# One block of a feed-forward product, instead of two, goes pair by pair: a transformer step on one core

## The chip, the core and the metric

The kernel runs on one core of one Trainium2 chip, in one launch. The metric is device time in microseconds (us). Three runs of the kernel before gave a median of 1669.56 us (1669.26 to 1672.01). Engines are named as in the profile: PE multiplies matrices, ACT and DVE are the scalar and the vector engine, POOL is GpSimd, and SP's queue issues most of the transfers (ACT issues some).

## What is computed

The reference is one layer of a diffusion backbone on 1152 tokens (1024 latent, 128 context) of width 1024, all in float32. Cut to what matters here:

```python
mix = (sigmoid(ga) * attn + sigmoid(gc) * conv) @ w_o           # 1024 x 1024
x = LN(ALPHA * x + g1 * mix)                                      # first norm
h = x * (1 + sc2) + sh2                                           # modulation
f = square(relu(h @ w1 + b1)) @ w2 + b2                           # 1024 -> 4096 -> 1024
x = LN(ALPHA * x + g2 * f)                                        # second norm
```

The change sits between `@ w_o` and the beginning of `h @ w1`; attention, convolution and the second product are not touched.

## The kernel before

**Float32 by parts.** PE multiplies a rounded format. Each float32 operand is cut into a high part (a copy on ACT) and a low part (a subtraction on DVE, source minus high part), and each product is three matmuls: high by high, high by low, low by high. So whatever PE reads has first been through one ACT and one DVE instruction.

**The wo passes.** The output projection goes over nine tiles of 128 tokens in three passes: half 0 of the columns for tiles 0 to 5, half 1 for tiles 0 to 8, half 0 for tiles 6 to 8 (`PASSES`). A tile is 8 x 3 matmuls of 512 columns. The weights of a pass are four entries of 512 KB, which come through a ring with two raw buffers and three buffers of parts (a fourth pair, `wo_last`, is given in for the last entry). `ring.load_to` loads an entry as soon as a raw buffer is free, which is when its last split (the DVE subtraction at line 122) has run. So of a pass's four entries two can be loaded ahead, and the other two only once the first two have been split; the splits of a new pass run beside the last tile of the pass before, as each entry's old parts come free.

**Work beside the passes.** `todo` is a list of closures with costs, written by hand; `spend(0.69)` after every third matmul runs as many as fit. They are: `ln1_sum` (lines 1046, 1047 and 1050 on DVE: gate, residual, statistics of half a tile), `ln1_apply` (norm of a tile: DVE and ACT by turns, two passes of ACT at line 1058), `turn` (four 128x128 transposes on PE at line 1112 into one bank, taken out with modulation by ACT at line 1122), and `combine` (the operands of the next stage: ACT's high parts at line 1130, DVE's low parts at line 1140 and sums at line 1144).

**The first feed-forward product** is done by a Strassen-Winograd scheme: both operands are quartered, and seven products (A11 B11, S1 T1, S2 T2, A12 B21, S3 T3, S4 B22, A22 T4, with S and T sums of quarters of the weights and of the tokens) take the place of eight. The hidden width is cut into 16 blocks j; the tokens into two pairs of quarter tiles of 288 columns. A product of one block with one pair is 12 matmuls. Products accumulate in four accumulators X, V, Z, W: in the order of `PARTS`, X, V, X, Z, X, V, W. After a product its accumulator is copied out (`keep`, ACT, line 1364) or added to a kept copy (`plus`, DVE, line 1367), and X and V go on accumulating afterwards, so the next product into X waits for the copy.

**The first blocks.** The operands of the second pair need tiles 4 to 8, so they come late. `AHEAD = 2` blocks are therefore done first with pair 0 alone and then with pair 1 alone: blocks 0 and 1 on pair 0, blocks 0 and 1 on pair 1, and blocks 2 to 15 with both pairs. Their weights' parts (14 products, hi and lo, 256 KB each) are cut long before, during the convolution stage, and kept in DRAM (`w1d`); each is loaded twice, once for each pair (line 1188). From block 2 on, `w1_load` (line 1173) loads the raw weights of a block, 1 MB, and sums and parts are made four products ahead (`w1_prep`, lines 824, 1195, 1196).

**Beside the four half blocks** run the rest of `todo`: the last norms, the turns of tiles 4 to 8 for pair 1 through two banks, and `combine(1)`, which is taken up product by product: `while pairs[-1] == 1 and made <= k`. Hidden results are squared (lines 1320, 1321), summed (line 1324) and spilled to DRAM by transfers that ACT issues.

Of the kernel before, what the change touches and what calls it, by code (L numbers as in the profile page):

```python
# [144 lines left out]
def emit(nc, tc, ctx, aps, outs):  # L145
# [654 lines left out]
    HALVES = (slice(0, 512), slice(512, 1024))  # L800
    WPARTS = ("A11", "S1", "S2", "A12", "S3", "S4", "A22")
# [8 lines left out]
    def w1_sum(u, pool):  # L810
# [9 lines left out]
        t = w1sum[j, 2] if name == "S4" else tmp(pool, [P, 512], "S1" if name == "S3" else name, 1)  # L820
# [6 lines left out]
    AHEAD = 2  # L827
    w1d = [dram.tile([P, 2, 512], F32, name=f"w1d{u}") for u in range(7 * AHEAD)]

    def w1_ahead():  # L830
# [9 lines left out]
        def high(u):  # L840
            if st:
                keep(u - 1)
# [8 lines left out]
        def keep(u):  # L851
            for i, x in enumerate(st.pop(u)):
                dma(w1d[u][:, i], f32(x))

        for j in range(AHEAD):
            bg.append(lambda j=j: load(j))
            for u in range(7 * j, 7 * j + 7):
                bg.extend([lambda u=u: high(u), lambda u=u: low(u)])
            bg.append(lambda: keep(max(st)))
# [229 lines left out]
    def place(pair, store):  # L1089
        for name in PARTS:  # L1090
            own = {"T4": "q00", "T3": "q10", "B22": "q01"}.get(name) if pair else None
            hx[pair][name] = (next(store), own or next(store))
# [11 lines left out]
    def turn(t, pair, half):  # L1104

        def go():
# [12 lines left out]
            for i in range(4):  # L1119
                kb = 4 * half + i  # L1120
                for x, y, n in pieces:
                    act(raw[pair][half][x // PT][:, i, x % PT:x % PT + n], b[:, i * P + y:i * P + y + n], AF.Identity,
                        scale=m2col[:, cond, 1, kb:kb + 1], bias=m2col[:, cond, 0, kb:kb + 1])
        return go

    def combine(pair):

        def high(name, src):
            for h_, k0, n in hx[pair][name][0]:
                nc.scalar.copy(h_, src[:, k0:k0 + n])  # L1130

        def low(name, src):
            hi, lo = hx[pair][name]
            if isinstance(lo, str):
                lo = [(tmp(rawp, [P, 4, PT], lo, 1, F32R), 0, 4)]
                hx[pair][name] = hi, lo
# [17 lines left out]
        if pair == 0:  # L1154
            first, second, third = cuts("B11", b11), cuts("B21", b21), cuts("B22", b22)
            t1, t3, t2, t4 = cuts("T1", b11), cuts("T3", b12), cuts("T2", b11), cuts("T4", b21)
            return ([first[0], second[0], first[1]] + sums(b11, b12, b11) + [t1[0], second[1], third[0], t1[1]]
                    + sums(b11, b22, b11) + [t2[0]] + sums(b21, b21, b11) + [t4[0], t2[1], third[1], t4[1]]
                    + sums(b12, b22, b12) + t3)
# [6 lines left out]
    BLOCKS = [(j, (p,)) for p in range(2) for j in range(AHEAD)] + [(j, (0, 1)) for j in range(AHEAD, NJ)]  # L1166
# [9 lines left out]
    def w1_prep(s_):  # L1176

        if s_ >= 7 * len(BLOCKS) or s_ in w1part:
            return
        j, k = BLOCKS[s_ // 7][0], s_ % 7  # L1180
        u = 7 * j + k
        if s_ // 2 not in wtile:
            wtile[s_ // 2] = [ringp.tile([P, 1024], F32R, tag=t, name=f"w1{t}{s_}", bufs=3) for t in ("whi", "wlo")]
        hi, lo = (t[:, HALVES[s_ % 2]] for t in wtile[s_ // 2])
        w1part[s_] = hi, lo
        if j < AHEAD:
            for i, x in enumerate((hi, lo)):
                dma(f32(x), w1d[u][:, i])
        else:
            w1_load(j)  # L1190
            w1_sum(u, wsp)
            if k < 6:
                w1_sum(u + 1, wsp)
            src = w1sum[j, k]
            nc.scalar.copy(hi, src)
            vec.tensor_tensor(out=lo, in0=src, in1=f32(hi), op=ALU.subtract)
        if k == 6 and s_ // 7 + 1 >= 2 * AHEAD:
            w1_load(j + 1 if j >= AHEAD else AHEAD)
# [5 lines left out]


# [25 lines left out]
    def put_turn(t, pair):  # L1231
        todo.extend((0.4, turn(t, pair, half)) for half in range(2))

    for ps, (half, ts_) in enumerate(PASSES):
        if ps == 0:
            ring.given[ring.nuse + 3] = wo_last(f"o{ps}")
        w = [ring.take(ahead=0) for _ in range(4)]
        for t in ts_:
# [7 lines left out]
            for kb in range(KB):  # L1246
# [4 lines left out]
                if t == ts_[-1] and kb % 2:  # L1251
                    if ps == 2:
                        if kb < 7:
                            w1_prep(kb - 1)
                            w1_prep(kb)
                    else:
                        if kb == 7:
                            ring.given[ring.nuse + 3] = wo_last(f"o{ps + 1}")
                        ring.split_to(ring.nuse + kb // 2 + 1)
                        ring.load_to(len(seq))  # L1260
                        room[0] -= 1.2
                spend(0.69)
# [4 lines left out]
            if ps == 1 and 1 <= t < 6:  # L1267
                put_turn(t - 1, 0)
            if ps == 1 and t == 5:
                store = segments(act_tiles(0) + act_tiles(1), 0)  # L1270
                store = list(store) + [single(hx0, n) for n in range(4)]
                place(0, iter(store))
                todo.append((0.0, lambda: todo.extendleft(reversed(combine(0)))))
# [4 lines left out]
    for _ in range(2):  # L1278
        todo.popleft()[1]()
    put_turn(7, 1)  # L1280
    put_turn(8, 1)
# [5 lines left out]
    turn_banks.extend(lambda i=i: bank(i) for i in (6, 7))  # L1287
# [9 lines left out]
    def dbank(tag, j, pairs):  # L1297

        if len(pairs) == 1:
            return bank("XVZW".index(tag)).rearrange("p (a b) -> p a b", a=1)  # L1300
        return ps1.tile([P, 2, 512], F32, tag=tag, name=f"d{tag}{j}", bufs=1)

    def w1_mm(b, s_, name, first, pairs):

        hi, lo = w1part[s_]
# [29 lines left out]
    def second_pair():  # L1335

        nonlocal made
# [3 lines left out]
        place(1, iter(store + [single(hx1, 4 + n) for n in range(6)]))  # L1341

        def count():
            nonlocal made
            made += 1

        for closures in combine(1):
            todo.extend(closures + [(0.0, count)])

    store = list(segments(act_tiles(2), 0))  # L1350
    todo.append((0.0, second_pair))
    B = {}
    for n, (j, pairs) in enumerate(BLOCKS):
        sl = slice(pairs[0], pairs[-1] + 1)
        bias = [b1c[:, j + i * NJ:j + i * NJ + 1] for i in range(2)]
        c1, c5, c2, c3 = (ht(t, n)[:, sl] for t in ("c1", "c5", "c2", "c3"))
        h = {m: ht("h" + m, n)[:, sl] for m in ("11", "22", "12", "21", "T2", "T3", "T4")}
# [11 lines left out]
        def spill(name, t, j=j, sl=sl):  # L1369
            nc.scalar.dma_start(hd[name, j][:, sl], t)  # L1370

        def finish(h=h, j=j, sl=sl, spill=spill):
# [5 lines left out]
            def parts(name, t):  # L1378
                hi = tmp(t1p, [P, 2, PT], "hi" + name, 1, F32R)[:, sl]
                nc.scalar.copy(hi, t)  # L1380
                vec.tensor_tensor(out=t.bitcast(F32R), in0=t, in1=f32(hi), op=ALU.subtract)
                late.append(lambda: (nc.scalar.dma_start(hd[name, j][:, sl, 0], f32(hi)),
                                     nc.scalar.dma_start(hd[name, j][:, sl, 1], t)))
# [10 lines left out]
        for k in range(7):  # L1394
            s_ = 7 * n + k
# [4 lines left out]
            while pairs[-1] == 1 and made <= k and todo:  # L1400
                todo.popleft()[1]()
# [8 lines left out]
            elif k == 3:  # L1410
                plus(h["11"], b, c1)
            elif k == 4:
                keep(c3, b, 1)
                plus(h["22"], b, c5)
            elif k == 5:
                plus(h["12"], b, c2)
            elif not last:
                plus(h["21"], b, c3)
            if last and k == 6:
                break  # L1420
            if todo:
                spend(1.3)
# [3 lines left out]
            elif k == 4:  # L1426
                after(lambda h=h, spill=spill: (square(h["22"]), spill("B11", h["11"])))
# [434 lines left out]
```

## Time and profile before

| | us |
|---|---|
| median of three runs | 1669.56 |
| the profiled execution | 1671.68 |
| its span | 1669.9 |
| PE busy | 1599.8 |
| DVE busy | 1026.0 |
| ACT busy | 734.8 |
| POOL busy | 201.4 |

The span counts from the first to the last instruction of the profiled execution; the run's own time lies 1.8 us above it. PE's matmuls overlap, so its busy share is no measure of its speed: the spacing of starts is. A wait names what ended it. In the views a line number is that of the kernel before.

### The profile page before, as it was taken

The numbers are of one execution on the slowest core, as the hardware profiler recorded it, in microseconds if no ns is written. First come the engines' busy times: TensorE is split into PE (matmuls) and PEld (weight loads), VectorE is DVE, ScalarE is ACT, GpSimd is POOL, SyncE is SP. The second block draws the span as 40 slices with busy tenths as digits, with TensorE's granted clock in tenths as the row PEclk, the third lists the DMA queues.
The fourth block names the chain that finished last, engine by engine and source line by source line (L and its number), as shares of the span: only waits on it lengthen the run. The fifth ranks groups of instructions, "written<-read, shape, count | busy, mean of one in ns | idle before, by whom it ended". The sixth has DMA issues, their size and how long they took to land.

```text
span 1669.9 us, 27468 instructions
## 1 busy us (share of the span) xinstructions
PE 1599.8 (96%) x10432; PEld 1539.7 (92%) x10432; DVE 1026.0 (61%) x1793; ACT 734.8 (44%) x1408; POOL 201.4 (12%) x214
## 2 busy tenths in 40 slices
PE   7999999999999999999987799999999999999995
PEld 5799999999999999997767799999999999999995
DVE  6568888665565554345464555666666457865666
ACT  5367777511112122232557555655565335453030
POOL 2145556100000002210000000000000121000002
PEclk9999999999999999999998999999999999999998
DMA  8432222133332223533326845444557898777792
GB/s 313 143 90 73 57 62 54 57 114 108 108 95 80 79 76 91 175 102 120 132 89 222 293 143 171 153 168 160 171 174 273 292 327 277 228 258 237 230 328 88
DMA packets 157419, 267.63 MB, mean 160 GB/s; under 512 B 41392, under 2 KB 62000, under 8 KB 157288
## 3 DMA queue, kind: packets, MB, share of 16 engines
q1 hardware_dynamic: 125352, 218.68, 40.9%
q10 hardware_dynamic: 31936, 47.21, 7.9%
q8 instruction: 82, 1.34, 0.3%
q14 instruction: 49, 0.40, 0.1%
HBM read 198.94 MB, written 66.88 MB: 159 GB/s over the span
## 4 chain that ended last, share of the span: by engine, by line
PE 77%; DVE 8%; DMA 5%; ACT 5%; issue 3%; SPq 1%; POOL 0%; ACTq 0%; POOLq 0%; DVEq 0%
PE ps L363 8%; PE ps L365 8%; PE ps L361 7%; PE pq L1552 6%; PE pq L1553 6%; PE pq L1554 6%; PE dX L1312 3%; PE dX L1314 3%; PE dX L1313 3%; PE dV L1312 2%; PE dV L1314 2%; PE dV L1313 2%; PE ps L880 2%; PE ps L881 2%; PE ps L882 2%
## 5 line engine op out<-in xcount | busy, mean ns | idle before, releaser
L365 PE MATMUL ps<-ahi,wl 128*128 128x384 f32 x864 | 292.7, 339 | 0.9 <-DVE wl L122 0.9
L363 PE MATMUL ps<-alo,wh 128*128 128x384 f32 x864 | 292.5, 339 | 0.0
L361 PE MATMUL ps<-ahi,wh 128*128 128x384 f32 x864 | 292.5, 339 | 0.0
L1552 PE MATMUL pq<-xh,vh 128*128 128x288 f32 x640 | 190.3, 297 | 3.2 <-ACT accc L1647 2.6
L1553 PE MATMUL pq<-xl,vh 128*128 128x288 f32 x640 | 189.5, 296 | 0.0
L1554 PE MATMUL pq<-xh,vl 128*128 128x288 f32 x640 | 188.9, 295 | 0.0
L365 PEld LDWEIGHTS ps<-ahi,wl 128*128 128x128 f32 x864 | 162.5, 188 | 1.7 <-DVE wl L122 1.5
L361 PEld LDWEIGHTS ps<-ahi,wh 128*128 128x128 f32 x864 | 162.4, 188 | 1.4 <-issue 0.2
L363 PEld LDWEIGHTS ps<-alo,wh 128*128 128x128 f32 x864 | 162.5, 188 | 0.8
L1552 PEld LDWEIGHTS pq<-xh,vh 128*128 128x128 f32 x640 | 120.6, 188 | 3.7 <-ACT accc L1647 2.8
L1554 PEld LDWEIGHTS pq<-xh,vl 128*128 128x128 f32 x640 | 121.2, 189 | 0.0
L1553 PEld LDWEIGHTS pq<-xl,vh 128*128 128x128 f32 x640 | 120.7, 189 | 0.0
L1519 DVE TENSOR_TENSOR xl<-hraw,xh 128x576 fp32r<-128x576 f32 x80 | 60.4, 755 | 77.4 <-ACT xh L1515 77.2
L122 DVE TENSOR_TENSOR wl<-wr,wh 128x1024 fp32r<-128x1024 f32 (+1 forms) x54 | 60.9, 1130 | 70.2 <-ACT wh L109 69.9
L1515 ACT CAST xh<-hraw 128x576 fp32r<-128x576 f32 x80 | 53.8, 673 | 96.7 <-issue 39.1
L1699 POOL TENSOR_TENSOR xm<-xm,ag 128x1024 f32<-128x1024 f32 x9 | 22.5, 2497 | 607.6 <-DMA w2r<-w 545.0
L743 DVE SCALAR_TENSOR_TENSOR acc<-wmb,sil,acc 128x512 f32<-128x512 f32 x112 | 78.2, 748 | 12.3 <-DMA wmb<-wmb 12.2
L109 ACT CAST wh<-wr 128x1024 fp32r<-128x1024 f32 (+1 forms) x62 | 58.2, 950 | 46.9 <-PE ps L1250 28.7
L1312 PE MATMUL dX<-hxahi,w1whi 128*128 128x288 f32 x224 | 67.5, 301 | 5.5 <-DVE h L1367 5.5
L563 ACT ACTIVATE s<-s,st 128x512 f32<-128x512 f32 (+1 forms) x72 | 49.6, 689 | 51.7 <-DVE st L561 51.1
L1314 PE MATMUL dX<-hxahi,w1wlo 128*128 128x288 f32 x224 | 67.0, 299 | 0.0
L881 PE MATMUL ps<-acl,wh 128*128 128x384 f32 x192 | 64.2, 334 | 0.0
(351 smaller groups left out, 4355.2 us busy)
## 6 DMA issues: line engine op xcount, KB each, us to landing
w2r<-w SPq DMA_DIRECT2D x144, 256.0 KB
hraw<-hdT SPq DMA_DIRECT2D x60, 288.0 KB
wmb<-wmb SPq DMA_DIRECT2D x64, 256.0 KB
w1r<-w SPq DMA_DIRECT2D x28, 512.0 KB
hraw<-hdB SPq DMA_DIRECT2D x44, 288.0 KB
hdB<-h ACTq DMA_DIRECT2D x42, 288.0 KB
hdT<-hT ACTq DMA_DIRECT2D x42, 288.0 KB
mr<-wma SPq DMA_DIRECT2D x16, 512.0 KB
```

What stands on the lines that cost most here:

```text
L122: engine.tensor_tensor(out=lo[:, :w], in0=self.raw.pop(i)[:, :w], in1=hi.bitcast(F32)[:, :w], op=ALU.subtract)
L361: mm(b[:, :CH], lhsT=hi[:, ws], rhs=a[0][:, kb, :], start=first and kb == 0, stop=False)
L363: mm(b[:, :CH], lhsT=hi[:, ws], rhs=a[1][:, kb, :], start=False, stop=False)
L365: mm(b[:, :CH], lhsT=lo[:, ws], rhs=a[0][:, kb, :], start=False, stop=last and kb == n - 1)
L743: vec.scalar_tensor_tensor(out=a, in0=t, scalar=sil[:, k, cond:cond + 1], in1=a, op0=ALU.mult, op1=ALU.add)
L881: mm(b[:, :CH], lhsT=hi[:, ws], rhs=parts[kb][1][:, cs_], start=False, stop=False)
L1312: mm(o, lhsT=hi[:, ws], rhs=xh, start=first and kb == 0, stop=False, **kw)
L1313: mm(o, lhsT=hi[:, ws], rhs=xl, start=False, stop=False, **kw)
L1314: mm(o, lhsT=lo[:, ws], rhs=xh, start=False, stop=kb == 3, **kw)
L1552: mm(o, lhsT=hi[:, ws], rhs=xh[:, i], start=j == 0, stop=False)
L1553: mm(o, lhsT=hi[:, ws], rhs=xl[:, i], start=False, stop=False)
L1554: mm(o, lhsT=lo[:, ws], rhs=xh[:, i], start=False, stop=j == NJ - 1)
```

## The change

Only block 0 goes pair by pair: block 0 on pair 0, block 0 on pair 1, then blocks 1 to 15 with both pairs. Its seven products' weight parts are cut early and kept in DRAM as before, but loaded once: six products fill the ring's three buffers, the seventh lies in two tiles that the hidden results use later. The products of every block come in a new order (`ORDER`: A11 B11, A12 B21, S1 T1, S2 T2, S4 B22, S3 T3, A22 T4), hence the accumulators in the order X, Z, V, X, V, X, W. Raw weights of wo's third and fourth entry are loaded into tiles of the hidden results (`wo_more`), which are free until then. Half, or a quarter, of the evictions of each turn move from ACT to DVE (`n_vec`), the turns of the first feed-forward stage use four banks instead of two, the cuts of pair 0's B11 and B21 begin after tile 3 instead of tile 5, no work is handed out during the last tile of the first two passes, and what goes beside each product of block 0 on pair 0 is written out (`beside`). Squares, sums and spills of block 0 are done once for both pairs.

```diff
+    ORDER = (0, 3, 1, 2, 5, 4, 6)
...
-        t = w1sum[j, 2] if name == "S4" else tmp(pool, [P, 512], "S1" if name == "S3" else name, 1)
+        t = tmp(pool, [P, 512], {"S4": "S1", "S3": "S2"}.get(name, name), 1)
...
-    AHEAD = 2
-    w1d = [dram.tile([P, 2, 512], F32, name=f"w1d{u}") for u in range(7 * AHEAD)]
+    w1d = [dram.tile([P, 2, 512], F32, name=f"w1d{u}") for u in range(7)]
...
-    def turn(t, pair, half):
+    def turn(t, pair, half, n_vec=0):
...
+                    if i < 4 - n_vec:
+                        act(to_, from_, AF.Identity, scale=sc, bias=sh)
+                    else:
+                        vec.tensor_scalar(out=to_, in0=from_, scalar1=sc, scalar2=sh, op0=ALU.mult, op1=ALU.add)
...
-        return [cuts("B11", b11), sums(b11, b12, b11) + cuts("T1", b11), sums(b11, b22, b11) + cuts("T2", b11),
-                cuts("B21", b21) + sums(b21, b21, b11), sums(b12, b22, b12) + cuts("T4", b21) + cuts("T3", b12),
-                cuts("B22", b22), []]
+        t1, t2, t3, t4, b = cuts("T1", b11), cuts("T2", b11), cuts("T3", b12), cuts("T4", b21), cuts("B22", b22)
+        return [cuts("B11", b11), cuts("B21", b21),
+                sums(b11, b12, b11) + [t1[0], b[0]] + sums(b12, b22, b12) + [t1[1]],
+                sums(b11, b22, b11) + [t2[0], b[1], t2[1]] + sums(b21, b21, b11) + [t4[0]], [], [t4[1]] + t3, []]
-    BLOCKS = [(j, (p,)) for p in range(2) for j in range(AHEAD)] + [(j, (0, 1)) for j in range(AHEAD, NJ)]
+    BLOCKS = [(0, (0,)), (0, (1,))] + [(j, (0, 1)) for j in range(1, NJ)]
...
+        if s_ < 7 or 14 <= s_ < 7 * len(BLOCKS):
...
+            if j == 0:
+                for x, t in enumerate((hi, lo)):
+                    dma(f32(t), w1d[k][:, x])
+                return
...
+    def wo_more(set_):
+        for e in (2, 3):
+            n = base + 4 * set_ + e
+            k, half = 2 * e, (0, 1, 0)[set_]
+            ts_ = [tmp(t1p, [P, 2, PT], "h" + ("11", "22", "12", "21")[2 * (e - 2) + x], 1)
+                   .rearrange("p a b -> p (a b)")[:, :512] for x in range(2)]
+            for x, t in enumerate(ts_):
+                dma(t, aps["wo"][k + x][:, HALVES[half]])
+            wo_raw[n] = ts_
...
+        for x, y in zip(src, HALVES):
+            nc.scalar.copy(hi[:, y], x)
+            vec.tensor_tensor(out=lo[:, y], in0=x, in1=f32(hi)[:, y], op=ALU.subtract)
...
-        w = [ring.take(ahead=0) for _ in range(4)]
+        w = [wo_take() for _ in range(4)]
+        if ps < 2:
+            wo_more(ps + 1)
+        else:
+            w1_load(1)
...
-                spend(0.69)
+                if ps == 2 or t < ts_[-1]:
+                    spend(0.69)
+                elif kb == 0:
+                    todo.popleft()[1]()
+                    room[0] = -1.0
...
-    turn_banks.extend(lambda i=i: bank(i) for i in (6, 7))
+    turn_banks.extend(lambda i=i: bank(i) for i in (0, 1, 6, 7))
...
+    beside = {0: [fn for _, fn in todo], 1: [last_norm, turn(7, 1, 0, 2), turn(7, 1, 1, 2), lambda: pair_parts(0)],
+              2: [lambda: pair_parts(1)],
+              3: [turn(8, 1, 0, 2), turn(8, 1, 1, 2), second_pair], 4: [lambda: pair_parts(2)],
+              5: [lambda: pair_parts(3)]}
...
-            while pairs[-1] == 1 and made <= k and todo:
-                todo.popleft()[1]()
+            while n == 1 and made <= min(i + 1, 6):
+                pair_parts(made)
...
+            if n == 0:
+                for fn in beside.get(i, ()):
+                    fn()
+                continue
```

More of the change, by code (lines that the diff above doesn't have):

```diff
@@ L849, in low, with keep_all @@
             vec.tensor_tensor(out=lo, in0=w1sum[u // 7, u % 7], in1=f32(hi), op=ALU.subtract)
[L851 to L859, printed above, removed]
+        def keep_all():
+            while st:
+                u, parts = st.popitem()
+                for i, x in enumerate(parts):
+                    dma(w1d[u][:, i], f32(x))
+        bg.append(lambda: load(0))
+        for u in ORDER:
+            bg.extend([lambda u=u: high(u), lambda u=u: low(u)])
+        bg.append(keep_all)
     gemv_rest()
@@ L1087, in act_tiles, with place @@
         return [actp.tile([P, KB * CH], F32R, tag=tag, name=f"hx{tag}{n}", bufs=NCH) for tag in ("ahi", "alo")]
[L1089 to L1092, printed above, removed]
+    def place(pair, store, names=PARTS):
+        for name in names:
+            own = ({"T4": (None, "q00"), "T3": ("q10", "q11")} if pair else {}).get(name, (None, None))
+            hx[pair][name] = tuple(x or next(store) for x in own)
     def single(pool, n):
@@ L1231, in put_turn @@
     def put_turn(t, pair):
-        todo.extend((0.4, turn(t, pair, half)) for half in range(2))
+        n_vec = 2 if not pair or t > 5 else 1
+        todo.extend((0.4 * n_vec, turn(t, pair, half, n_vec)) for half in range(2))
     for ps, (half, ts_) in enumerate(PASSES):
@@ L1268, in emit @@
                 put_turn(t - 1, 0)
+            if ps == 1 and t == 3:
+                store = list(segments(act_tiles(0), 0))
+                place(0, iter(store), ("B11", "B21"))
+                todo.append((0.0, lambda: todo.extendleft(reversed(combine(0)[0]))))
             if ps == 1 and t == 5:
[L1270 to L1273, printed above, removed]
+                store = store[4:] + list(segments(act_tiles(1), 0)) + [single(hx0, n) for n in range(4)]
+                place(0, iter(store), [x for x in PARTS if x not in ("B11", "B21")])
+                todo.append((0.0, lambda: todo.extendleft(reversed(combine(0)[1]))))
                 put_turn(4, 1)
@@ L1277, in emit @@
                 put_turn(6, 1)
-    for _ in range(2):
-        todo.popleft()[1]()
-    put_turn(7, 1)
-    put_turn(8, 1)
+    todo.popleft()[1]()
+    last_norm = todo.popleft()[1]
     sln.close()
@@ L1335, in second_pair @@
     def second_pair():
-        nonlocal made
         spill_x()
@@ L1378, in parts @@
             def parts(name, t):
[L1379 removed]
+                hi = tmp(t1p, [P, 2, PT], "hi" + name, 1, F32R)
                 nc.scalar.copy(hi, t)
                 vec.tensor_tensor(out=t.bitcast(F32R), in0=t, in1=f32(hi), op=ALU.subtract)
[L1382 to L1383 removed]
+                late.append(lambda: (nc.scalar.dma_start(hd[name, j][:, :, 0], f32(hi)),
+                                     nc.scalar.dma_start(hd[name, j][:, :, 1], t)))
             parts("B21", h["21"])
@@ L1392, in sums @@
             diff(h["T2"], h["22"], h["12"])
-        for k in range(7):
-            s_ = 7 * n + k
+        for i, k in enumerate(ORDER):
+            s_ = 7 * n + i
             new = {0: "X", 1: "V", 3: "Z", 6: "W"}.get(k)
```

140 lines of the change are left out of this document (88 added, 52 removed).

## The prediction

> **What bounds the kernel now.** I began with the page: who is busy, and at what clock.
>
> ```profile
> span 1669.9 us, 27468 instructions
> PE 1599.8 (96%) x10432; PEld 1539.7 (92%) x10432; DVE 1026.0 (61%) x1793; ACT 734.8 (44%) x1408; POOL 201.4 (12%) x214
> PEclk9999999999999999999998999999999999999998
> ```
>
> PE is the bound, and the number of its matmuls doesn't change. The change can therefore only give back time in which PE stood or ran at a lower clock. The next view is busy time by stretch: the three wo passes, the four half blocks (cut in two), the beginning of block 2, and blocks 2 to 15. The columns are PE, weight loads, DVE, ACT, POOL, the granted clock, the DMA share and GB/s.
>
> ```profile
> 762.90:801.00 38.10, 35.01 (x145) 27.99 (x145) 20.24 (x28) 5.13 (x6) 1.52 (x2) 0.96 0.35 118
> 801.00:857.70 56.70, 55.17 (x258) 44.43 (x256) 28.92 (x49) 34.27 (x74) 0.00 (x0) 1.00 0.40 138
> 857.70:880.80 23.10, 18.78 (x72) 13.96 (x72) 17.62 (x25) 8.03 (x10) 0.00 (x0) 0.93 0.35 106
> 880.80:920.00 39.20, 30.15 (x175) 28.18 (x173) 16.80 (x26) 31.18 (x76) 0.00 (x0) 0.83 0.63 216
> 920.00:958.40 38.40, 28.66 (x206) 27.33 (x204) 20.11 (x35) 18.51 (x39) 0.00 (x0) 0.99 0.90 306
> 958.40:964.20 5.80, 5.75 (x24) 5.75 (x25) 5.08 (x10) 2.84 (x6) 0.00 (x0) 0.51 0.39 122
> 964.20:1264.00 299.80, 299.80 (x2253) 299.80 (x2253) 184.17 (x277) 175.35 (x282) 0.00 (x0) 1.00 0.47 161
> ```
>
> From 964 on PE never stands; all that the change can save lies between 763 and 964. To see how much, I need PE's undisturbed pace. These are rows of the timeline (two successive tiles of a wo pass, then the first matmul of two blocks that lie 12 apart) and, third, one turn pair from the chain of waits.
>
> ```profile
> 779.30 0.69 DVE L1046 TENSOR_TENSOR lnt<-ps,g 128x512 f32<-128x512 f32 x1 [3.35 <-PE ps L1250]
> 784.81 0.69 DVE L1046 TENSOR_TENSOR lnt<-ps,g 128x512 f32<-128x512 f32 x1 [3.36 <-PE ps L1250]
> ...
> 817.43 0.87 PE ps L1112 x8
> ...
> 983.44 0.29 PE L1312 MATMUL dX<-hxahi,w1whi 128*128 128x288 f32 x1
> 1251.92 0.29 PE L1312 MATMUL dX<-hxahi,w1whi 128*128 128x288 f32 x1
> ```
>
> A tile takes 5.5, the eight transposes of one turned tile 0.87, a block (1251.92 - 983.44) / 12 = 22.37, a half block 11.19, one product of a half block 1.6 and of a whole one 3.2. Work against time, stage by stage:
> - pass 0: 6 tiles 33.0 of 38.1, lost 5.1
> - pass 1: 9 tiles and 5 turns 53.9 of 56.7, lost 2.8
> - pass 2: 3 tiles 16.5 of 23.1, lost 6.6
> - four half blocks and 5 turns: 44.7 + 4.4 = 49.1 of 77.6, lost 28.5
> - block 2, from 958.45 to 983.44: 25.0 for 22.4, lost 2.6
>
> Together 45.6. The waits of PE and the chain of waits over this stretch say why:
>
> ```profile
> PE ps L1312 <- ACT c L1364: 8.7, 4, 2.9
> PE dX L1312 <- DVE h L1367: 5.5, 1, 5.5
> PE ps L1249 <- DVE wl L122: 4.6, 4, 2.4
> PE ps L1112 <- ACT q L1122: 3.8, 3, 1.7
> PE ps L1248 <- ACT wh L109: 3.2, 4, 1.7
> ```
>
> ```profile
> 763.64 1.95 DVE alo L204 x3
> ...
> 800.91 4.36 DMA wr<-wo
> ...
> 861.84 4.68 DMA wr<-wo
> ...
> 925.20 5.19 DMA w1wlo<-w1d
> ...
> 947.40 6.25 DMA w1r<-w
> ...
> 958.45 0.61 PE dX L1312
> ```
>
> Pass 0 waits for the cuts of its input (line 204). Passes 1 and 2 wait for raw wo weights (800.91, 861.84). The half blocks wait first for ACT (copies of accumulators behind turn evictions), then, with the transfer engines 90% busy, for the twice loaded weights and last for block 2's raw weights. The waits named sum to 26 of the 45.6; much of the rest is the clock, which is below 1.00 in five of the seven stretches, down to 0.51.
>
> **The change, part by part.**
>
> *wo's raw weights in free tiles.* Pass 0's 5.1 stay: its entries come as before, and line 204 is untouched. For passes 1 and 2 the raw data are there a whole pass (33 and 50 us) ahead of the 4.4 and 4.7 that they took. Then only the splits are left, one entry per quarter of the last tile (1.4 us); they run on ACT and DVE, from which other work is kept in that tile, except the sum of the tile before. Pass 1: 2.8 becomes 0.3 (bounds 0 and 2.8). Pass 2: DVE comes to it with pair 0's cuts still queued, so 1.5 remain (bounds 0.5 and 4). Gain 2.5 + 5.1 = 7.6. The eight added transfers of 256 KB replace four of 512 KB, and stand on SP's queue ahead of token loads that run tiles ahead; I cost them at nothing, and at 1 us a pass if that lead is gone.
>
> *Weights loaded once.* 14 transfers of 256 KB instead of 56 go past SP's queue beside the half blocks, and 14 instead of 28 writes before. The 90% stretch goes, and with it the last waits of the third and fourth half block. Block 1's raw weights are loaded at the start of pass 2, so the 5.5 before the first whole block go too. The first loads can't start before pass 2's last tile frees its buffers; 1 us is left there.
>
> *One half block as cover instead of two.* This is the price. Everything that pair 1 needs must be made beside block 0 on pair 0, 11.2 us, and while its own half block runs. I add up DVE's list from the end of pass 2 to the low part of T3, by rows of the timeline:
>
> ```profile
> 811.81 0.21 DVE L1036 BATCH_NORM_AGGREGATE bag<-bst 128x2 f32<-128x12 f32 x1
> ...
> 812.58 0.21 DVE L1039 TENSOR_SCALAR bag<-bag 128x1 f32<-128x1 f32 x1
> ...
> 922.03 0.45 DVE L1367 TENSOR_TENSOR h<-ps,c 128x288 f32<-128x288 f32 x1
> 922.40 1.35 DVE L1140 TENSOR_TENSOR hxs<-q,hxs 128x1152 fp32r<-128x1152 f32 x1
> ...
> 925.66 1.35 DVE L1144 TENSOR_TENSOR q<-q,q 128x1152 f32<-128x1152 f32 x1
> 926.93 0.45 DVE L1367 TENSOR_TENSOR h<-ps,c 128x288 f32<-128x288 f32 x1
> ...
> 819.35 2.87 ACT L1122 ACTIVATE q<-ps,m2col 128x128 f32<-128x128 f32 x8
> ```
>
> ```profile
> 1020.77 0.69 DVE L824 TENSOR_TENSOR S<-w1r 128x512 f32<-128x512 f32 x1 [2.37 <-DMA w1r<-w]
> 1021.38 0.68 DVE L1196 TENSOR_TENSOR w1wlo<-w1r,w1whi 128x512 fp32r<-128x512 f32 x1
> 1023.85 0.75 DVE L1367 TENSOR_TENSOR h<-dX,c 128x576 f32<-128x576 f32 x1
> ...
> 1021.80 0.29 PE L1312 MATMUL dV<-hxs,w1whi 128*128 128x288 f32 x1
> ```
>
> - tile 8's sum, three instructions of 0.7: 2.1
> - its norm, 811.81 to 812.79: 1.0
> - eleven cuts and sums of 1152 columns, start to start 1.27 (925.66 to 926.93): 14.0
> - five accumulator sums of 288 columns, 0.37 each (922.03 to 922.40): 1.9
> - three weight sums and parts for block 1, 0.61 each (1020.77 to 1021.38): 1.8
> - the turn evictions that are new on DVE. Counting the costs in `todo`, the turns of tiles 5 and 6 are left at the end of pass 2, then come 7 and 8: 2 + 8 + 4 + 4 = 18. Before shows no such instruction. Between 288 and 1152 columns a column costs (1.27 - 0.37) / 864 = 1.04 ns, which leaves 0.07 fixed: 0.2 for 128 columns, 3.6 in all. Upper bound is the whole 0.45 of a 288 column row, 8.1; lower, the 0.36 that each takes from ACT (2.87 / 8) shortens the chain by more than DVE pays, so 3 below nothing. I take 3.6, the row's slope.
>
> [...]
>
> The list is 24.4 of busy time. To it come waits on ACT, as DVE runs its queue in order. In the half blocks of before the same cuts waited this much (the last column but the releaser):
>
> ```profile
> L1140 DVE TENSOR_TENSOR hxahi<-q,hxahi 128x576 fp32r<-128x576 f32 (+1 forms) x2 | 2.1, 1053 | 3.8 <-ACT hxahi L1130 3.8
> L1140 DVE TENSOR_TENSOR hxalo<-q,hxalo 128x576 fp32r<-128x576 f32 (+1 forms) x2 | 2.1, 1055 | 0.9 <-ACT hxalo L1130 0.9
> L1140 DVE TENSOR_TENSOR q<-q,hxs 128x1152 fp32r<-128x1152 f32 x3 | 4.1, 1356 | 1.0 <-ACT hxs L1130 0.9
> ```
>
> 5.7; and I add 2.5 for tile 8's norm, whose ACT step stands behind the leftover evictions (14 x 0.36 less what DVE does meanwhile), 1.4 for T3 (its high part goes into the tile that T4's low part reads, then 1.05 on ACT and a handover), and 2 for block 1's first high part, queued behind two squares. That is 11.6, and T3 is ready 36 us after pass 2. PE, undisturbed, would come to it after 84 + 60 matmuls and four turns: 19.2 + 3.5 = 22.7. So PE stands 13 us in the two half blocks, mostly waiting for accumulator copies and T3. The windows with clock 0.83 and 0.51 show what such waits drag behind them; I add 3.5 (half clock for 7 us), together 17 with rounding. Bounds: 6, if the waits on ACT vanish (24.4 - 22.7 and one slow stretch of 4), and 29, if evictions cost 0.45 and the waits double (13 + 4.5 + 11.6; the slow clock then falls into the waits).
>
> So in place of 28.5 + 2.6 lost, 17 + 1: gain 13 (bounds 1 and 24).
>
> [...]
>
> *The new order.* X is used by products 1, 4, 6 and then 1 of the next block: one product (3.2) between the sixth and the next, where there were two. I cost it at nothing: the row at 1023.85 is a late such sum, ending 1024.6, 2.8 after its product (which ended at 1021.80). If that cover is gone it is lost 15 times; see below.
>
> **The sum.** 7.6 + 13 = 20.6; from the profiled execution's 1671.7 that leaves 1651.1. The median of the runs lies 2.1 lower than that execution: 1649.
>
> **The rivals.**
> - *Cover too thin*: evictions at 0.45 and longer waits (29 lost), gain 7.6 + 1, 1661. For it: DVE's list is 24.4 against 22.7 of PE's work before any wait. Against it: ACT is relieved, and four banks replace the two on which line 1112 waited 3.8.
> - *Slower, by the new order.* Place: the sum of X after S3 T3 in blocks 1 to 15. At 1020.77 DVE stands 2.37 for raw weights, and 1023.85 stands behind it. If that wait fell right ahead of the sum, it would come 2.8 + 2.4 = 5.2 after its product against 3.2: 2 us in 15 blocks, 30; 1649 + 30 = 1679. It decides from 1.4 us a block (21 / 15). Against it: S1, the first sum to need those weights, is now prepared two products before that sum.
> - *The wo loads don't help*: the splits stay late, DVE being behind; gain 13 alone, 1656.6.
> - *Everything hidden*: 6 lost, pass losses near nothing, gain 7.6 + 24 = 32, 1638.
>
> **How the numbers follow.** Forecast 0.57 (its own range 1641 to 1657), cover too thin 0.17, wo loads 0.08, all hidden 0.11, slower 0.07. A difference under 0.2% (3.3 us) can't be told from none here. The first gives, at its far end, 0.03 of no change, from the case of thin cover. So faster 0.90, same 0.03, slower 0.07. The range 1637 to 1662 leaves out the slower case, some of the thin cover and of the hidden one. I predict 1649.
>
> **What would show it.** Right: no wait on DMA at the starts of passes 1 and 2; transfers well below 90% in the half blocks; PE waiting for `c` (line 1364's) and T3's low part there, some 13 us; whole blocks at 22.4 from block 2 on. Wrong: whole blocks longer than 22.4 (the order), waits for raw weights at the first whole block, or half blocks over 53 us together with turns.

## The result, and the profile after

The changed kernel takes 1657.36 us (median of four runs, 1656.38 to 1658.67) against 1670.60 for the kernel before in the same session. The ratio is 0.9921, with a 95% interval from 0.9904 to 0.9938: 13 us faster. Forecast were 1649, within 1637 to 1662. The profiled execution took 1657.08, forecast 1651.1. From here on the line numbers are those of the changed kernel: wo's matmuls are lines 1318 to 1320, transposes 1113, matmuls of the first feed-forward product 1388 to 1390, turn evictions 1126 (ACT) and 1128 (DVE), cuts 1140 (high) and 1147 (low), sums of tokens 1151, splits of wo 109 and 122 (ring) and 1257 and 1258 (free tiles), copies of accumulators 1451 and sums onto them 1454.

The page of the changed kernel, busy time (its span is 1655.3).

```profile
PE 1594.0 (96%) x10432; PEld 1536.8 (93%) x10432; DVE 1046.2 (63%) x1826; ACT 717.2 (43%) x1344; POOL 201.8 (12%) x214
```

The same number of matmuls, more work on DVE, less on ACT. Busy time by stretch: pass 0, pass 1, pass 2, block 0 pair by pair with its five turns, the fifteen whole blocks, and the rest (columns as in the prediction).

```profile
761.30:799.50 38.20, 35.11 (x145) 28.11 (x144) 20.45 (x29) 6.27 (x8) 1.53 (x2) 0.96 0.41 145
799.50:853.50 54.00, 54.00 (x257) 44.27 (x255) 35.00 (x76) 25.44 (x50) 0.00 (x0) 1.00 0.44 146
853.50:878.00 24.50, 19.74 (x75) 15.34 (x74) 22.63 (x32) 11.07 (x15) 0.00 (x0) 0.86 0.32 109
878.00:921.70 43.70, 33.56 (x210) 31.93 (x209) 30.07 (x52) 27.30 (x56) 0.00 (x0) 0.85 0.27 96
921.70:1257.30 335.60, 335.60 (x2521) 335.56 (x2520) 210.10 (x310) 196.23 (x313) 0.00 (x0) 1.00 0.50 169
1257.30:1655.30 398.00, 373.73 (x2786) 370.43 (x2784) 268.25 (x419) 145.58 (x265) 31.67 (x15) 0.98 0.78 256
```

With the prediction's pace for each piece of work (tile 5.5, turn 0.87, block 22.37):

| stretch | lost before | forecast | lost after |
|---|---|---|---|
| pass 0 | 5.1 | 5.1 | 38.2 - 33.0 = 5.2 |
| pass 1 | 2.8 | 0.3 | 54.0 - 53.9 = 0.1 |
| pass 2 | 6.6 | 1.5 | 24.5 - 16.5 = 8.0 |
| half blocks | 28.5 | 17 | 43.7 - 26.7 = 17.0 |
| first whole block | 2.6 | 1 | 0 |
| sum | 45.6 | 24.9 | 30.3 |

So four rows came as forecast, and one went the other way: pass 2 got worse, 8.0 lost where it lost 6.6 before. Transfers are busy 27% of the half blocks, where they were at 63 and 90%, and from pass 1 to the whole blocks PE waits for no DMA. The last stretch holds the second product, which the change doesn't touch. Before, it read

```profile
1274.20:1669.90 395.70, 372.87 (x2786) 370.26 (x2785) 262.24 (x416) 144.09 (x261) 31.78 (x15) 0.98 0.78 257
```

2.3 less than after; and pass 0 starts 1.6 earlier (761.3 for 762.9). The whole difference of the spans is then 45.6 - 30.3 + 1.6 - 2.3 = 14.6, and so much do the spans differ (1669.9 and 1655.3).

Whole blocks first: two rows of PE's timeline, the first matmul of two blocks that lie 12 apart.

```profile
944.30 0.29 PE L1388 MATMUL dX<-hxahi,w1whi 128*128 128x288 f32 x1
...
1212.62 0.29 PE L1388 MATMUL dX<-hxahi,w1whi 128*128 128x288 f32 x1
```

(1212.62 - 944.30) / 12 = 22.36: the new order takes nothing from the whole blocks. What PE waits for in the half blocks (total, times, longest):

```profile
PE ps L1388 <- ACT c L1451: 3.8, 2, 2.2
PE ps L1388 <- ACT q L1140: 3.4, 1, 3.4
PE ps L1389 <- DVE q L1147: 1.0, 1, 1.0
PE ps L1388 <- DVE h L1454: 1.0, 1, 1.0
PE ps L1113 <- ACT xk L1059: 1.0, 1, 1.0
```

Together 10.2; it is `c` and the two parts of T3 (`q`), as forecast. At the start of pass 2 it is the split of its first entry:

```profile
PE ps L1318 <- ACT wh L109: 4.3, 1, 4.3
PE ps L1319 <- DVE wl L122: 0.5, 1, 0.5
```

Of the 8.0 lost these are 4.8. The rest is the clock, 0.86 over the pass (0.50 from 860.0 to 864.2) against 0.93 before, where PE's waits in pass 2 came to 4.3.

Why is the split late, with the raw data long there? These are ACT's rows of the timeline around it:

```profile
854.52 1.15 ACT L1140 CAST hxahi<-q 128x1152 fp32r<-128x1152 f32 x1 [2.46 <-DVE q L1151]
855.91 1.15 ACT L1140 CAST hxs<-q 128x1152 fp32r<-128x1152 f32 x1 [0.24 <-DVE q L1151]
856.97 1.99 ACT L109 CAST wh<-wr 128x1024 fp32r<-128x1024 f32 x2
```

The split (line 109) waits for nothing of its own. Two high parts of pair 0's operands stand ahead of it in ACT's queue, and they wait for DVE's sums. And DVE's rows of the same timeline:

```profile
840.59 1.42 DVE L1128 TENSOR_SCALAR q<-ps,m2col 128x128 f32<-128x128 f32 x4 [2.28 <-ACT q L1126]
841.93 0.68 DVE L1047 TENSOR_TENSOR lnt<-ps,g 128x512 f32<-128x512 f32 x1
...
847.26 1.18 DVE L1128 TENSOR_SCALAR q<-ps,m2col 128x64 f32<-128x64 f32 x4 [2.18 <-ACT q L1126]
848.36 1.35 DVE L1151 TENSOR_TENSOR q<-q,q 128x1152 f32<-128x1152 f32 x1
...
853.13 2.75 DVE L1151 TENSOR_TENSOR q<-q,q 128x1152 f32<-128x1152 f32 x2
```

DVE's turn evictions here begin with waits of 2.3 and 2.2 for ACT's evictions of the same turn (in the whole of pass 1 five such waits, 11.8 in all); the first sum of pair 0 (848.36) comes behind them, and everything up to the split follows in order.

### The profile page after: what moved, and what is told of

It is laid out like the page before. It is cut to its first block, busy times and chain, and to the rows that moved or that the text cites. A ratio compares the mean times of both kernels' runs of the same rounds, so it can differ in the third digit from the quotient of the medians.

```text
span 1655.3 us, 27274 instructions
## 1 busy us (share of the span) xinstructions
PE 1594.0 (96%) x10432; PEld 1536.8 (93%) x10432; DVE 1046.2 (63%) x1826; ACT 717.2 (43%) x1344; POOL 201.8 (12%) x214
## 4 chain that ended last, share of the span: by engine, by line
PE 79%; DVE 8%; ACT 5%; issue 3%; DMA 3%; POOL 1%; SPq 0%; POOLq 0%; ACTq 0%; DVEq 0%
PE ps L363 8%; PE ps L365 8%; PE ps L361 8%; PE pq L1641 6%; PE pq L1643 6%; PE pq L1642 6%; PE dX L1388 3%; PE dX L1390 3%; PE dX L1389 3%; PE dV L1388 2%; PE dV L1390 2%; PE dV L1389 2%; PE ps L882 2%; PE ps L883 2%; PE ps L881 2%
## 5 line engine op out<-in xcount | busy, mean ns | idle before, releaser
L1604 ACT CAST xh<-hraw 128x576 fp32r<-128x576 f32 x80 | 53.9, 673 | 96.4 <-issue 44.5
L1788 POOL TENSOR_TENSOR xm<-xm,ag 128x1024 f32<-128x1024 f32 x9 | 22.4, 2484 | 593.3 <-DMA w2r<-w 532.7
L1451 ACT ACTIVATE c<-dX,b1c 128x576 f32<-128x576 f32 x45 | 33.3, 741 | 73.1 <-PE dX L1390 73.1
L883 PE MATMUL ps<-ach,wl 128*128 128x384 f32 x192 | 64.2, 334 | 0.0
```

Source lines behind the costliest of these rows:

```text
L883: mm(b[:, :CH], lhsT=lo[:, ws], rhs=parts[kb][0][:, cs_], start=False, stop=kb == 3)
```

## The experiments

Theory A: pass 2 waits because DVE and ACT are late, and they are late because the evictions that the change puts on DVE are ordered behind ACT's. Rivals: the splits are late for their data; the evictions' number or price is what counts; the work of both engines up to T3 is fixed, so that what is gained at one wait returns at the next.

**All evictions on ACT.** In `turn`:

```diff
-                    if i < 4 - n_vec:
+                    if True:
```

> Edit: all evictions of the turns go to ScalarE, as before the change; the rest of the changed kernel stays. Theory A (VectorE late by waiting): the 8.2 us lost at the start of pass 2 come from VectorE's queue, which is behind because its turn evictions stand until ScalarE has done its own of the same turn (15.4 us in 8 waits). Then the wait of 4.3 for wh goes, pass 2 loses 2 or less, the half blocks 13 to 20 as ScalarE takes 20 evictions of 0.44 more and VectorE none: 1648 to 1653. Rival R1 (transfers): the splits are late for their data, pass 2 still loses 8, time 1657 or more. Rival R2 (conserved): what pass 2 gains comes back as longer half blocks, since the work of both engines up to T3 is the same: 1656 to 1659. Rival R3 (ScalarE needs the relief): copies of accumulators stand behind the evictions, half blocks lose over 25: over 1660.

1658.3 us, ratio 0.9929 (0.9915 to 0.9942): no change that can be measured, and theory A's 1648 to 1653 missed. Pass 2's wait for `wh` fell from 4.3 to 2.3 only. First DVE's row of this kernel, then ACT's:

```profile
847.48 1.36 DVE L1151 TENSOR_TENSOR q<-q,q 128x1152 f32<-128x1152 f32 x1 [2.76 <-ACT q L1126]
```

```profile
856.10 1.99 ACT L109 CAST wh<-wr 128x1024 fp32r<-128x1024 f32 x2
```

The sum waits for the evictions itself, since it reads what they write. It is 0.9 earlier than in the changed kernel (847.48 for 848.36), and so is the split (856.10 for 856.97). So what counts is when a turn's last eviction ends, and with ACT doing all eight in a row that is nearly as late as with the two engines one behind the other. What pass 2 gains comes back on both sides of it: pass 1 takes 55.3 instead of 54.0, pass 2 22.8 instead of 24.5, the half blocks 45.5 instead of 43.7, where PE's waits grew from 10.2 to 14. Moving evictions to DVE the way the change does it is thus worth 1 us or nothing.

**As many on DVE, but of the other half of the tile.**

```diff
-                    if i < 4 - n_vec:
+                    if i < 4 - 2 * n_vec * half:
```

> Edit: as many turn evictions on VectorE as in the changed kernel, but all of them from the second half of the turned tile, so that the two engines write different tiles from different banks (of the turns with two per half; those with one per half give two of the second). Theory A: VectorE no longer stands for ScalarE's evictions, its 15.4 us of such waits fall below 5, it comes to the end of pass 1 some 4 us earlier, pass 2 loses 4 or less: 1650 to 1654. If the waits only followed from ScalarE being late with other work, or the durations of 0.41 are what matters, nothing changes: 1656 to 1658.

1653.32 us, ratio 0.9898 (0.9884 to 0.9912): about 4 less than the changed kernel, with intervals that overlap a little. The trace shows where. DVE, then ACT:

```profile
844.29 1.36 DVE L1151 TENSOR_TENSOR q<-q,q 128x1152 f32<-128x1152 f32 x1 [1.76 <-ACT q L1126]
```

```profile
852.91 1.99 ACT L109 CAST wh<-wr 128x1024 fp32r<-128x1024 f32 x2
```

Sum and split are both 4.1 earlier than in the changed kernel (0.3 of it because pass 1 began so much earlier). Pass 2 takes 18.4 instead of 24.5, at clock 1.00; the half blocks take the same 43.7.

**The same evictions, VectorE's queued first.**

```diff
-            for i in range(4):
+            for i in (3, 2, 1, 0):
```

> Edit to the changed kernel: in each half of a turn the evictions are queued from the last to the first, so that VectorE's come before ScalarE's; number and place stay. Theory A says that VectorE stands because its evictions are ordered behind ScalarE's of the same tile, though both only read what the transposes left. If that order follows from the queueing, it turns round: VectorE's 15.4 us of waits for ScalarE fall below 4, it comes to the end of pass 1 some 4 us earlier, pass 2 loses 4 or less: 1651 to 1654. If VectorE is held by something else of ScalarE (the token tile's norm ahead of it): 1656 to 1658.

1650.62 us, ratio 0.9881 (0.9867 to 0.9896), below the changed kernel's interval. What ended DVE's idle time ahead of line 1128 (us, times), in the changed kernel:

```profile
  ACT q L1126: 15.4, 8
```

and here, with the same 44 evictions:

```profile
  PE ps L1113: 0.8, 2
...
  ACT q L1126: 2.0, 2
```

The last row is the other way round: ACT now waits for DVE, 2.0 in all. The split follows:

```profile
854.84 1.99 ACT L109 CAST wh<-wr 128x1024 fp32r<-128x1024 f32 x2
```

That is 53.1 after the beginning of pass 1 (801.7), where the changed kernel needs 57.4 (799.5 to 856.97). Pass 2 takes 17.8. So the order in which the two engines' evictions of half a turn are queued decides who stands, though they write different columns; ACT, which also has the token tile's norm (line 1059) ahead of its evictions, should come second. This is theory A, and with it the rivals of data and of price fall.

What orders the two? They share the tile that they write and the bank that they read. One turn of the changed kernel, whose 128 tokens are split between two operand tiles (32 and 96 columns), tells these apart. ACT's last two evictions of one bank, then DVE's first:

```profile
829.64 0.37 ACT L1126 ACTIVATE q<-ps,m2col 128x32 f32<-128x32 f32 x1
829.91 0.43 ACT L1126 ACTIVATE q<-ps,m2col 128x96 f32<-128x96 f32 x1
```

```profile
830.37 0.31 DVE L1128 TENSOR_SCALAR q<-ps,m2col 128x32 f32<-128x32 f32 x1 [2.77 <-ACT q L1126]
```

DVE's first writes the tile of the 32 columns. ACT's last write into that tile ended at 830.01, its last into the other at 830.34, and DVE starts 0.03 after the latter. So the common tile isn't what held DVE here. The bank that both read fits, but a run that gives the two engines one tile from two banks is missing.

**Pair 0's cuts behind the splits.**

```diff
-                todo.append((0.0, lambda: todo.extendleft(reversed(combine(0)[1]))))
-                put_turn(4, 1)
-                put_turn(5, 1)
...
         else:
             w1_load(1)
+            todo.append((0.0, lambda: todo.extendleft(reversed(combine(0)[1]))))
+            put_turn(4, 1)
+            put_turn(5, 1)
```

> Edit: all of pair 0's cuts but the first four, and the two turns behind them, are queued at the beginning of pass 2 instead of after tile 5 of pass 1, so behind the splits for pass 2. Theory A: nothing is left in front of the splits, the wait of 4.3 goes and pass 2 loses 2 or less; the five or so cuts that ran in pass 1 now stand in pass 2 and beside the half blocks, 6 us more of VectorE there: half blocks lose 20 to 24, time 1653 to 1658. R1 (transfers): pass 2 loses 8 as before and the half blocks more: over 1662. R2 (conserved): 1657.

1657.25 us, ratio 0.9919 (0.9907 to 0.9931): the same as the changed kernel. Its stretches of pass 2 and of block 0 pair by pair:

```profile
853.60:870.00 16.40, 16.40 (x72) 13.19 (x71) 14.99 (x22) 7.48 (x10) 0.00 (x0) 1.00 0.41 131
870.00:922.00 52.00, 35.48 (x209) 33.90 (x209) 37.13 (x61) 29.24 (x59) 0.00 (x0) 0.80 0.24 86
```

Pass 2 loses nothing at all, and the half blocks take 52.0 instead of 43.7: all 8 come back. Here the third rival holds: work that is only moved from in front of one wait to in front of the next gains nothing. The two runs before gained because they took waiting out of the queue, and not work.

**wo's free tiles undone.** The calls of `wo_more` go, and `wo_load` loads every entry through the ring:

```diff
-        if ps < 2:
-            wo_more(ps + 1)
-        else:
+        if ps == 2:
             w1_load(1)
...
-            if ring.nload >= base + 4 and (ring.nload - base) % 4 >= 2:
-                ring.nload += 1
-            else:
-                ring.load_to(ring.nload + 1)
+            ring.load_to(ring.nload + 1)
```

> Edit: wo's raw weights in free tiles undone: all four entries of each pass come through the two ring buffers, as before the change. By the forecast's term the free tiles give 7.6 us: 1665. Theory A: pass 2 would lose its 8.2 anyway, since the splits are late for VectorE; only pass 1 loses its 2.8 again, and a little at pass 2, where the two waits lie one beside the other: 1659 to 1661. If raw data were not late either way: 1657.

1662.67 us, ratio 0.9952 (0.9940 to 0.9964): 5.3 over the changed kernel. Passes 1 and 2 of this kernel:

```profile
799.80:856.80 57.00, 55.23 (x258) 44.13 (x256) 35.27 (x74) 26.40 (x50) 0.00 (x0) 1.00 0.42 138
856.80:882.80 26.00, 20.32 (x73) 15.15 (x73) 20.64 (x26) 9.27 (x10) 0.00 (x0) 0.87 0.41 124
```

Pass 1 takes 3.0 more than in the changed kernel, pass 2 only 1.5 more: there the data's lateness lies beside that of the engines.

**The same, where the engines aren't late.** The last diff in the kernel with VectorE's evictions first, so that both are in it:

```diff
-            for i in range(4):
+            for i in (3, 2, 1, 0):
...
-            if ring.nload >= base + 4 and (ring.nload - base) % 4 >= 2:
...
+            ring.load_to(ring.nload + 1)
```

> Edit: the kernel with VectorE's evictions queued first, 1650.6, and wo's free tiles undone in it. Theory A: in the changed kernel the free tiles gave 5.3 instead of the forecast's 7.6, because pass 2's splits were late anyway. Here they aren't late, so both passes pay for the missing tiles, 2.8 and 4 to 5: 1657.5 to 1659.5. Rival (the free tiles are worth 5 whatever the splits do): 1655 to 1656.5.

1657.93 us, ratio 0.9935 (0.9922 to 0.9948), 7.3 over the 1650.62 of the kernel that keeps the tiles. The free tiles are worth about what the prediction gave them, 7.6, once the splits don't wait for something else; in the changed kernel two or three of it are lost. The two medians come from different sessions, and by the ratios the difference is 9.0 and not 7.3, with intervals too wide to tell it from 5.3. The traces tell them apart: without the free tiles, passes 1 and 2 together take 79.3 instead of 71.9 here (2.5 more in pass 1, 5.0 in pass 2), and 83.0 instead of 78.5 in the changed kernel.

**The old order of products in the whole blocks.** The order and the tags of the weight sums depend on the block:

```diff
     ORDER = (0, 3, 1, 2, 5, 4, 6)
+    ORD = lambda j: tuple(range(7)) if j else ORDER
...
-        for i, k in enumerate(ORDER):
+        for i, k in enumerate(ORD(j)):
```

> Edit: the 15 whole blocks take their seven products and sums of weights in the old order; block 0 keeps the new one. The prediction costed the new order at nothing: blocks stay at 22.37 us and the time at 1657. Rival (the new order delays sums of X): blocks below 22.36 are not possible, so the time can't fall by it but for the 2.3 us that the second product's beginning lost against before (1257.5 to its end 397.8, before 395.6); if these come from the new order's last block, 1655.

1654.78 us, ratio 0.9912 (0.9898 to 0.9926): not to be told from the changed kernel. PE's first matmuls of two blocks 12 apart start at 943.47 and 1212.11: 22.39 for a block. In this run the second product takes 398.3, so its 2.3 us more are not the new order's. In the next run, whose second product is that of the kernel before, it takes 399.1; with 395.7 in the profiled execution of before, the same code spreads over 3.4 us, and I leave those 2.3 as scatter between executions.

**One block instead of two alone.** The kernel before, with one number changed:

```diff
-    AHEAD = 2
+    AHEAD = 1
```

> Edit, made to the kernel before: one block instead of two goes pair by pair, its weights still stored once and loaded twice, everything else as before. Theory T (transfers): what bounded the four half blocks were the 56 transfers of twice loaded weights, 90% busy; two half blocks then lose about half of the 31 us, gain 10 to 15: 1656 to 1660, and the new schedule of cuts was not needed. Theory C (cover): with the old schedule pair 1's cuts don't fit beside one half block, so PE stands for them; gain 0 to 5: 1665 to 1671.

1675.82 us, ratio 1.0035 (1.0023 to 1.0047): slower than the kernel before, and worse than both theories gave. Its profiled execution, 1680.69, is the slowest of six. The two half blocks in two parts:

```profile
882.70:915.00 32.30, 23.40 (x149) 21.05 (x148) 12.16 (x19) 26.17 (x68) 0.00 (x0) 0.92 0.70 234
915.00:944.20 29.20, 16.45 (x62) 14.53 (x62) 16.61 (x22) 12.30 (x22) 0.00 (x0) 0.62 0.26 93
```

61.5 us for one block and its turns, where the changed kernel takes 43.7. What PE waits for there (the two largest of ten rows):

```profile
PE ps L1313 <- DVE hxs L1140: 5.0, 2, 4.5
PE ps L1312 <- ACT hxs L1130: 4.6, 2, 3.0
```

Cuts, and a third row with 4.4 for turn evictions; on transfers of the stored weights PE waits 0.6. Together with whole blocks 1 and 2 that is 61.5 + 22.4 + 22.4 = 106.3, where the four half blocks and block 2 of before took 77.6 + 25.0 = 102.6. So in this stretch the halving alone costs some 4; another 2 of this execution lie in pass 2, at clock 0.87 for 0.93. Halving the half blocks thus gains nothing under the schedule of before. The gain needs the new one (cuts and turns written out beside each product, four banks, weights loaded once). Which of its parts pays isn't shown: of them I tried only the evictions alone. Nor is it shown what the new schedule would gain with two blocks.

**Pair 1's cuts ahead of the next block's weights.** The changed kernel's T3 is ready when these rows are done, first DVE's, then ACT's:

```profile
910.21 0.69 DVE L1212 TENSOR_TENSOR w1wlo<-w1r,w1whi 128x512 fp32r<-128x512 f32 x1 [1.98 <-ACT w1whi L1211]
...
911.42 0.69 DVE L1212 TENSOR_TENSOR w1wlo<-w1r,w1whi 128x512 fp32r<-128x512 f32 x1
912.02 1.35 DVE L1147 TENSOR_TENSOR q<-q,hxs 128x1152 fp32r<-128x1152 f32 x1
914.59 1.36 DVE L1147 TENSOR_TENSOR q<-q,q 128x1152 fp32r<-128x1152 f32 x1 [1.22 <-ACT q L1140]
```

```profile
913.41 1.15 ACT L1140 CAST q<-q 128x1152 fp32r<-128x1152 f32 x1 [2.32 <-DVE q L1147]
```

Three instructions for block 1's weights, with a wait of 1.98 in front, stand ahead of T4's low part (912.02), T3's high part (913.41) goes into the tile that this one reads, and T3's low part (914.59) follows. Queued the other way, in the kernel with evictions by half:

```diff
-            w1_prep(s_ + 4)
-            while n == 1 and made <= min(i + 1, 6):
+            while n == 1 and made <= min(i + (2 if i > 2 else 1), 6):
                 pair_parts(made)
+            w1_prep(s_ + 4)
```

> Edit: as in the run with evictions by half, and beside block 0's pair 1 the cuts come ahead of the preparation of block 1's weights, T4's low part and T3 one product earlier. Theory: the wait of 3.4 and 0.8 for T3 is one of order, since its cuts stand behind five instructions for block 1's weights and behind a copy of an accumulator that ScalarE has to do first; it goes to under 1.5, and with it some of the slow clock: 1648 to 1650. Rival (both engines' work up to the first whole block bounds): PE then waits as long for block 1's weights, 1652 to 1655.

1647.31 us, ratio 0.9864 (0.9850 to 0.9877), 6.0 below the run with evictions by half. T3's low part runs at 905.69, where it ran at 908.55 in that run; PE waits for T3 no more, block 1's weights are in time, and the half blocks take 37.6 instead of 43.7. PE's waits in them fall from 11.3 to 7.4; the rest is the clock, 0.95 for 0.88.

**This edit alone**, in the changed kernel (the diff just shown).

> Edit to the changed kernel: the earlier cuts of T4 and T3 alone, evictions as in the changed kernel. If the two repairs are independent (pass 2's start, and T3), this one alone gives what it gave on top of the evictions by half, 6: 1650 to 1652, with pass 2 still losing 8. If it works only when VectorE is not behind: 1654 to 1657.

1651.79 us, ratio 0.9892 (0.9878 to 0.9907); pass 2 and the half blocks of this kernel:

```profile
853.60:877.90 24.30, 19.58 (x75) 15.11 (x75) 22.76 (x32) 11.08 (x15) 0.00 (x0) 0.86 0.34 111
877.90:915.20 37.30, 30.88 (x210) 29.25 (x209) 28.48 (x49) 26.01 (x54) 0.00 (x0) 0.91 0.29 104
```

Pass 2 as bad as ever, the half blocks 6.4 shorter: the two repairs are independent.

**B11's cut of pair 1 behind T1's accumulator copy**, with evictions by half and the earlier cuts:

```diff
-    beside = {0: [fn for _, fn in todo], 1: [last_norm, turn(7, 1, 0, 2), turn(7, 1, 1, 2), lambda: pair_parts(0)],
-              2: [lambda: pair_parts(1)],
+    beside = {0: [fn for _, fn in todo], 1: [last_norm, turn(7, 1, 0, 2), turn(7, 1, 1, 2)],
+              2: [lambda: pair_parts(0), lambda: pair_parts(1)],
```

> Edit to the kernel with both repairs: the first cut for pair 1 (B11) comes after product T1's accumulator copy instead of before it. The wait of 2.2 for c at 887.4 has ScalarE's high part of that cut and the norm of tile 8 ahead of the copy; 1.0 of it goes, and perhaps the slow clock behind it (3 us at half clock, 1.5): 1645 to 1646.5. If VectorE's chain to T3 decides, T3 comes later by as much and the time stays at 1647 to 1648.

1646.71 us, ratio 0.9864 (0.9844 to 0.9883), not to be told from 1647.31. PE's wait of 2.2 for `c` became 1.1 and 0.6, but the one for `h` (line 1454) grew from 2.0 to 3.9: the wait moved.

**All together**: VectorE's evictions first, earlier cuts, B11 later.

> Edit to the changed kernel: VectorE's turn evictions queued first, the cuts of T4 and T3 earlier, B11's cut of pair 1 behind T1's accumulator copy. If the repairs are independent: 1657.4 less 6.8 (evictions queued first), less 6 (cuts earlier, measured on two kernels), less 0.6: 1644. If what is left of the half blocks is one chain through both engines, which each repair shortens at the same place: 1646 to 1648.

1645.06 us, ratio 0.9856 (0.9841 to 0.9871): 12 below the changed kernel and 24 below the kernel before. It lies between the two expectations. What PE still waits for from pass 2 to the first whole block:

```profile
PE ps L1388 <- DVE h L1454: 3.9, 1, 3.9
PE ps L1388 <- ACT c L1451: 2.3, 4, 1.1
```

With two smaller rows 7.4 in all, where the changed kernel has 15.

## Why the prediction was right, and where it was wrong

The sign and the range were right, and the forecast of 1649 was 8 us too low. 2.1 of these I took off for the median, on the ground that the profiled execution of before lay above it; the changed kernel's profiled execution lies at its median, and with more runs so does, within 1.1, that of before. The other 6.0 (1657.1 less 1651.1) are, within rounding, the table's 5.4 more lost and 2.3 in the second product, less 1.6 gained ahead of pass 0; the last two I did not forecast.

- *Passes 0 and 1*: 5.1 and 0.3 forecast, 5.2 and 0.1 found.
- *Pass 2* is the step that failed: "then only the splits are left", with 1.5 lost and 4 at most. 8.0 were lost, 4.8 by waits for the split; the rest, 3.2, I put down to the slow clock behind them (0.50 from 860.0 to 864.2). I saw that DVE comes to it with cuts queued, and counted their time on DVE. I did not follow ACT's queue, where the split stands behind two high parts that wait for DVE's sums, nor did I count the wait of the new evictions for ACT ahead of those sums. The rival *the wo loads don't help* named this mechanism, with 0.08; it came true for pass 2 and not for pass 1. That its 1656.6 lies within 1 us of the measured time is in part luck, as it has no gain in pass 1 and nothing for the second product. The 7.6 of this part were about the right worth of the free tiles (7.3 where splits aren't late), but not their worth here (5.3), and still less the gain of the two passes against before: 9.4 lost there, 8.1 here, so 1.3. Without the free tiles the changed kernel takes 83.0 for them and loses 12.6, so the rest of the change costs these passes some 3.
- *Half blocks*: 17 forecast, 17.0 found, and T3 ready 36 us after pass 2 against 38 (878.0 to 916). The sum is closer than its terms, which is luck. An eviction on DVE took 0.33 (840.59 to 841.93, four of them), neither my 0.2 nor the upper bound of 0.45, so the 20 of them, some narrower, cost about 6 where I had 3.6 for 18. Waits of PE are 10.2 for 13 forecast, and the rest is 6.8 for 3.5; the two stretches at half clock are some 5 of it, by the estimate in the last section. I listed the cause of T3's lateness (the high part that goes into T4's tile), but not that the order of the queue made it; it cost 6.
- *What the half blocks' gain rests on*: I argued from cover and took the schedule as given. With the schedule of before the same halving costs 6 (1675.8), some 4 of it in the half blocks and block 2. My rival *cover too thin* describes that kernel.
- *Weights loaded once, first whole block*: no wait for them, no wait at 921.7; as forecast, with the 1 us left over not needed.
- *The new order*: nothing forecast, nothing found (22.36 for a block, 22.39 in the old order). The slower rival didn't come about.
- *A reading*: I wrote that from 964 on PE never stands. The row ends at 1264; in the second product, which the change leaves, PE is busy 372.87 of 395.70.

## What to carry to other kernels

Follow a late instruction back through the queue of its own engine, and through every instruction ahead of it there, before crediting a transfer that it no longer waits for. When two engines share the evictions of one bank into one tile, queue the part of the engine that is free first ahead of the other's (1650.62 us here, for 1657.36), or give each a bank and a tile of its own (1653.32; the run by half changed both at once). Let operands that the matrix engine needs next go ahead of weights for the block after (1651.79 for 1657.36). Here taking a wait out of a queue gained time, while moving work from before one wait to before the next didn't (1657.25).

## What I had not expected of the hardware

The clock was low for longer than I had reckoned with: in block 0 it was 0.50 for twice 5.7 us, where I had added half clock for 7 us in all. These are stretches of the changed kernel at the first entries of pass 0 and in block 0 (columns as above, the granted clock third from the end):

```profile
764.70:768.50 3.80, 1.21 (x4) 0.80 (x5) 3.80 (x7) 1.21 (x2) 0.00 (x0) 1.00 0.19 70
768.50:772.00 3.50, 3.50 (x11) 2.72 (x10) 0.38 (x1) 0.00 (x0) 0.00 (x0) 0.51 0.86 259
...
889.00:892.60 3.60, 1.37 (x9) 0.90 (x9) 1.95 (x5) 3.60 (x8) 0.00 (x0) 0.84 0.39 146
892.60:898.30 5.70, 5.70 (x24) 5.70 (x25) 5.58 (x9) 3.17 (x7) 0.00 (x0) 0.50 0.02 3
...
916.00:921.70 5.70, 5.70 (x24) 5.70 (x25) 2.89 (x6) 2.62 (x5) 0.00 (x0) 0.50 0.12 48
```

In 764.7 to 768.5 PE is busy 1.21 of 3.80, with two waits of which the longer is 2.4, and then it runs at half clock for 3.5 us. At 889.0 to 892.6 it is busy 1.37 of 3.60, with a wait of 0.9 just ahead and one of 2.2 within, and half clock (0.50) follows to 898.3. So in both places idle time in pieces, none over 2.4, came before half clock. In the run with evictions by half and earlier cuts it didn't follow:

```profile
892.40:896.00 3.60, 1.60 (x13) 1.37 (x12) 3.53 (x6) 2.70 (x4) 0.00 (x0) 1.00 0.00 0
896.00:900.00 4.00, 4.00 (x30) 4.00 (x31) 4.00 (x4) 1.17 (x1) 0.00 (x0) 1.00 0.00 0
```

PE is busy 1.60 of 3.60, with a longest wait of 2.0, and the clock stays at 1.00. Nor was the clock the same after equal waits: pass 0, unchanged, with the same two waits of 0.7 and 2.4, takes 38.2 at clock 0.96 here, 36.7 at 1.00 in the runs *Pair 0's cuts behind the splits* and *B11's cut*, and 39.2 at 0.91 with VectorE's evictions first. What decides isn't shown; between these executions pass 0 differs by 2.5 us.

In the slow stretches of block 0 a matmul starts 0.24 after the one before, and 0.13 once the clock is back at 1.00:

```profile
894.11 0.44 PE L1388 MATMUL ps<-hxs,w1whi 128*128 128x288 f32 x1
894.35 0.44 PE L1389 MATMUL ps<-hxs,w1whi 128*128 128x288 f32 x1
...
898.64 0.29 PE L1390 MATMUL ps<-hxs,hiT 128*128 128x288 f32 x1
898.77 0.29 PE L1388 MATMUL ps<-hxs,hiB 128*128 128x288 f32 x1
```

For the 48 matmuls of the two stretches that makes, as an estimate, 48 x 0.11 = 5 of their 11.4 us, about as much as the two longest waits of block 0, 3.4 and 2.2. The half blocks lose 17.0 in all, 10.2 of it by waits; what the other 1.5 or so of the remaining 6.8 went to isn't shown.
